# Retention values and gates of a hybrid layer computed as seven block products instead of eight, from block sums of the normalised tokens

## The chip, the cores and the metric

The kernel runs on one core of a Trainium2 chip. The metric is the device time of one execution in microseconds (us). A core has a matrix engine (TensorE, PE in the profile; its weight loads are shown apart as PEld), a vector engine (VectorE, DVE), an activation engine (ScalarE, ACT), GpSimd (POOL) and SyncE (SP). Each engine works through its own instructions in the order in which they stand in its queue; semaphores tie the queues together. SP issues most of the DMA transfers, POOL those that add into their target.

## The reference, cut to what matters

One decoder layer on 512 tokens of width 1024. Of its products with weights, these belong to the retention branch:

```python
h = rms_norm(x, norm_mix)
proj = h @ w_in
rq, rk, rv, rg, cq, ckv, krope, gr, gm = jnp.split(proj, offsets, axis=-1)
rq = rope(rq.reshape(B, S, RET_HEADS, RET_QK_DIM), pos)            # 4 heads of 256
rk = rope(rk.reshape(B, S, RET_HEADS, RET_QK_DIM), pos) * (RET_QK_DIM ** -0.5)
rv = rv.reshape(B, S, RET_HEADS, RET_V_DIM)                        # 4 heads of 512
ro = retention(rq, rk, rv)                                         # decayed causal scores times values
ro = rms_norm(ro, ret_norm.reshape(RET_HEADS, RET_V_DIM)).reshape(B, S, RET_V_W)
a_ret = (ro * jax.nn.silu(rg)) @ w_br
...
mixed = jax.nn.sigmoid(gr) * a_ret + jax.nn.sigmoid(gm) * a_mla
x = x + mixed @ w_o
h2 = rms_norm(x, norm_mlp)
x = x + jnp.square(jax.nn.relu(h2 @ w_up)) @ w_down
```

The values `rv` and the gates `rg` are each a product of the normalised tokens (512 x 1024) with 1024 x 2048 weights. The rest is a latent attention branch (`a_mla`), the output projection `w_o`, the MLP and a gated per-layer embedding.

## The kernel before, in words

**Products.** Tokens lie along the free dimension, features on the 128 partitions. Every float32 product is made of three matmuls on operands split into a high and a low part (`mm3`, L160 to L168; all matmuls are recorded at L165). A split is an ACT copy to the high part and a DVE subtraction that gives the low part (L294 and L295 for activations; L254 and L255 for weights).

**Weights** are streamed in chunks of 128 x 1024 (512 KB). `prepare` (L215 to L240) starts a chunk's transfer on SP into a ring of raw tiles (NRAW = 3), three steps ahead (PREP = 3). `load_chunk` (L243) splits it into a ring of three high and three low tiles (NW = 3), one step ahead (AHEAD = 1). A split therefore waits until the matmuls that used the ring's tile three chunks earlier are done. The order of the work is written out by hand as a list of steps at the end of the kernel (from L1058); one step is one chunk of weights and the matmuls on it. The tile framework orders the work of the engines other than PE from this list.

**The retention stage** is a loop over four heads after the eight `bm` chunks, which project the attention output. For one head h:
- `rq` and `rk`, two chunks each (heads 1 to 3; head 0's run earlier), and four chunks `br` that project the head before;
- `rv`, four chunks (`ret_v`, L692): 24 matmuls a chunk with 128 tokens stationary and 512 weight columns moving;
- the scores `rs` (L705), and `rg` chunks 0 and 1 (`ret_gate`, L743): 24 matmuls a chunk with 128 x 128 weights stationary and 512 tokens moving;
- `ro` (`ret_attend`), `rg` chunk 2, then `so`, the sums of squares of `ro` (`ret_stats`), and `rg` chunk 3;
- between `so` and `pbo`, DVE forms 1/sqrt of the sums in 12 small instructions on 128 x 4 (`mean_rsqrt` and `rsqrt`, L311 to L316, L393). `pbo` (`ret_factor`) is the PE instruction that spreads the result `ro0` over the partitions, and DVE multiplies it into `og` (L741).
- The gate `rg` is multiplied by the tokens' norm factor `rbc` on DVE (`z`, L746), goes through ACT's sigmoid (`sg`, L747) and is multiplied by itself (L748).

The tokens are used as `xg`, which carries the gain but not the norm factor; the factor is multiplied in afterwards (into `rv` as a scale of the split, into `rg` and `gr` by DVE).

**Seven products for eight.** The product with `w_down` (`dn`) already uses a form in which a 2 x 2 block product takes 7 block products of sums of blocks instead of 8: the activations' sums are made on DVE (`combine`), the weights' sums by transfers issued on POOL that add a second chunk into a raw tile that holds the first (L225). The products are numbered 1, 7, 6, 2, 5, 4, 3; the weights of 7, 6, 4 are one tile that is added to twice more, so that its next addition has to wait until the last split has read it.

## Time and profile before

| what | before |
|---|---|
| time, median of 3 runs | 1145.36 us (1144.82 to 1145.98) |
| the profiled execution: time, span of the core | 1144.94 us, 1143.2 us |
| PE, DVE, ACT, POOL busy | 1120.1, 700.0, 484.9, 29.1 us |
| PE instructions | 5300 matmuls, 5300 weight loads in the trace |
| granted TensorE clock, mean | 0.999 |
| DMA | 133.42 MB, mean 117 GB/s |

How to read it: the busy time of PE is near to the span, but matmuls overlap in the pipeline (one of 512 columns is recorded as 0.39 us and the next starts 0.23 us later), so the share says that PE hardly ever stands still and not that its array is full. The chain of work that ended last follows back, from the end, what each step waited for. In a timeline, the first number of a row is its start, the second its recorded duration, and "idle before" how long the engine stood still and what ended it.

### The profile page before, as it was taken

The numbers are of one execution on the slowest core, as the hardware profiler recorded it, in microseconds if no ns is written. First come the engines' busy times: TensorE is split into PE (matmuls) and PEld (weight loads), VectorE is DVE, ScalarE is ACT, GpSimd is POOL, SyncE is SP. The second block draws the span as 40 slices with busy tenths as digits, with TensorE's granted clock in tenths as the row PEclk, the third lists the DMA queues.
The fourth block names the chain that finished last, engine by engine and source line by source line (L and its number), as shares of the span: only waits on it lengthen the run. The fifth ranks groups of instructions, "written<-read, shape, count | busy, mean of one in ns | idle before, by whom it ended". The sixth has DMA issues, their size and how long they took to land.

```text
span 1143.2 us, 13662 instructions
## 1 busy us (share of the span) xinstructions
PE 1120.1 (98%) x5300; PEld 935.0 (82%) x5300; DVE 700.0 (61%) x1138; ACT 484.9 (42%) x682; POOL 29.1 (3%) x38
## 2 busy tenths in 40 slices
PE   7998999999999999999999999999999999999998
PEld 5887878888888888888888888878888888888877
DVE  5777676653448247644834666545566566668675
ACT  6546556452334343233324333424444343445542
POOL 0000000000000000000000000000100001001000
PEclk9999999999999999999999999999999999999999
DMA  6223131233312321331232133676657657667221
GB/s 201 73 69 111 38 89 45 66 111 98 116 56 90 107 89 59 98 117 56 87 110 90 49 105 117 202 248 203 129 167 195 136 175 192 144 204 195 67 90 73
DMA packets 43344, 133.42 MB, mean 117 GB/s; under 512 B 5296, under 2 KB 6576, under 8 KB 43024
## 3 DMA queue, kind: packets, MB, share of 16 engines
q1 hardware_dynamic: 38400, 115.36, 30.5%
q0 software_dynamic: 4736, 17.18, 8.7%
q8 instruction: 41, 0.67, 0.2%
q14 instruction: 23, 0.19, 0.0%
q10 hardware_dynamic: 144, 0.03, 0.0%
HBM read 126.25 MB, written 4.19 MB: 114 GB/s over the span
## 4 chain that ended last, share of the span: by engine, by line
PE 93%; DVE 3%; DMA 2%; ACT 1%; issue 0%; SPq 0%; ACTq 0%; DVEq 0%
PE up L165 15%; PE dn L165 13%; PE rg L165 8%; PE br L165 8%; PE rv L165 8%; PE pg L165 4%; PE rq L165 4%; PE rk L165 4%; PE gr L165 4%; PE bm L165 4%; PE gm L165 3%; PE ro L165 3%; PE wo L165 2%; PE sc L165 2%; PE pcq L165 1%; PE rs L165 1%
## 5 line engine op out<-in xcount | busy, mean ns | idle before, releaser
L254 ACT ACTIVATE wh_dp<-dr 128x1024 fp32r<-128x1024 f32 x56 | 59.4, 1061 | 117.5 <-PE up L165 83.2
L255 DVE TENSOR_TENSOR wl_dp<-dr,wh_dp 128x1024 fp32r<-128x1024 f32 x56 | 68.4, 1221 | 49.9 <-ACT wh_dp L254 49.9
L165 PE MATMUL dn<-wh_dp,cl 128*128 128x512 f32 x224 | 87.2, 389 | 0.0
L165 PE MATMUL dn<-wh_dp,ch 128*128 128x512 f32 x224 | 87.2, 389 | 0.0
L165 PE MATMUL dn<-wl_dp,ch 128*128 128x512 f32 x224 | 87.2, 389 | 0.0
L254 ACT ACTIVATE wh_up<-wr_up 128x1024 fp32r<-128x1024 f32 x32 | 33.9, 1061 | 58.7 <-PE up L165 29.3
L225 POOL DMA_DIRECT2D dr<-wstream x32 | 27.6, 873 | 1028.5 <-DMA dr<-wstream 894.2
L255 DVE TENSOR_TENSOR wl_up<-wr_up,wh_up 128x1024 fp32r<-128x1024 f32 x32 | 39.1, 1222 | 17.8 <-ACT wh_up L254 17.6
L165 PEld LDWEIGHTS dn<-wl_dp,ch 128*128 128x128 f32 x224 | 42.1, 188 | 8.7
L165 PEld LDWEIGHTS dn<-wh_dp,cl 128*128 128x128 f32 x224 | 42.1, 188 | 8.7
L165 PEld LDWEIGHTS dn<-wh_dp,ch 128*128 128x128 f32 x224 | 42.1, 188 | 8.6
L845 DVE SCALAR_TENSOR_TENSOR f<-up,bcx 128x512 f32<-128x512 f32 x32 | 20.6, 685 | 43.9 <-PE up L165 43.9
L255 DVE TENSOR_TENSOR wl_rg<-wr_rg,wh_rg 128x1024 fp32r<-128x1024 f32 x16 | 19.6, 1226 | 36.7 <-ACT wh_rg L254 36.7
L254 ACT ACTIVATE wh_rv<-wr_rv 128x1024 fp32r<-128x1024 f32 x16 | 17.0, 1060 | 55.3 <-PE br L165 26.2
L255 DVE TENSOR_TENSOR wl_rv<-wr_rv,wh_rv 128x1024 fp32r<-128x1024 f32 x16 | 19.6, 1226 | 32.8 <-ACT wh_rv L254 32.8
L254 ACT ACTIVATE wh_rg<-wr_rg 128x1024 fp32r<-128x1024 f32 x16 | 17.0, 1062 | 46.3 <-PE rv L165 35.0
L746 DVE TENSOR_TENSOR z<-rg,rbc 128x512 f32<-128x512 f32 x16 | 11.1, 691 | 39.8 <-PE rg L165 39.8
L254 ACT ACTIVATE wh_br<-wr_br 128x1024 fp32r<-128x1024 f32 x16 | 17.0, 1062 | 41.8 <-issue 18.8
L903 DVE TENSOR_TENSOR d<-d,dn 128x1024 f32<-128x1024 f32 x24 | 29.3, 1219 | 6.5 <-PE dn L165 6.5
L765 DVE TENSOR_TENSOR ret<-ret,br 128x512 f32<-128x512 f32 x24 | 16.5, 686 | 18.2 <-PE br L165 18.1
L622 ACT ACTIVATE p<-p,ng,hr 128x128 f32<-128x128 f32 (+3 forms) x32 | 20.7, 647 | 15.1 <-DVE ng L620 15.1
L255 DVE TENSOR_TENSOR wl_br<-wr_br,wh_br 128x1024 fp32r<-128x1024 f32 x16 | 19.5, 1217 | 3.6 <-ACT wh_br L254 3.6
(1590 smaller groups left out, 3376.9 us busy)
## 6 DMA issues: line engine op xcount, KB each, us to landing
dr<-wstream SPq DMA_DIRECT2D x40, 512.0 KB, 4.3
wr_up<-wstream SPq DMA_DIRECT2D x32, 512.0 KB, 4.2
dr<-wstream POOLq DMA_DIRECT2D x32, 512.0 KB, 5.8
wr_rv<-wstream SPq DMA_DIRECT2D x16, 512.0 KB, 3.4
wr_rg<-wstream SPq DMA_DIRECT2D x16, 512.0 KB, 3.4
wr_br<-wstream SPq DMA_DIRECT2D x16, 512.0 KB, 3.4
wr_gm<-wstream SPq DMA_DIRECT2D x16, 256.0 KB, 2.6
wr_bm<-wstream SPq DMA_DIRECT2D x8, 512.0 KB, 3.5
```

The lines of the kernel that those rows point to most:

```text
L165: return tc.keep_in_program_order(nc.tensor.matmul(*a, **k))
L225: nc.gpsimd.dma_start(raw, chunk(("d", gg, kb, fb, c)), accum_op=ALU.add)
L254: ACT(hi, raw, AF.Copy)
L255: TT(lo, raw, hi.bitcast(F32), op=ALU.subtract)
L622: ACT(cols[b], cols[b], AF.Exp, bias=ng[:, b:b + 1], scale=d["rq"][:, b], accum_out=sums[:, b:b + 1])
L746: TT(z, ps, V["rbc"], op=ALU.mult)
L765: TT(ret[n], ret[n], ps, op=ALU.add)
L845: STT(u[:, i], ps[:, i], 0.0, V["bcx2"], op0=ALU.max, op1=ALU.mult)
L903: TT(to, to, dps[p], op=ALU.add if sign > 0 else ALU.subtract)
```

## The change

**Values.** Two heads are computed together, as 2 x 2 blocks: token halves of 256 by halves of the 1024 features, and feature halves by the two heads' 512 columns. Seven products of two chunks each, 12 matmuls of 512 columns a chunk, for heads 0 and 1 ahead of head 0 and for heads 2 and 3 ahead of head 2. The `br` chunks of head 1 stand between the products of the second pair.

**Gates.** Per head, the 512 gate columns are split into two halves of 256 and the tokens too: seven products of one chunk each, 24 matmuls with 128 x 128 weights stationary and 256 tokens moving. Their order around the other work of the head is 1, 7, `rs`, 2, 6, `ro`, 5, `so`, 4, 3, `pbo`. `seven_out` gathers the results: products 1, 7 and 6 by an ACT copy out of PSUM, 2, 5 and 4 by a DVE addition, and product 3's sum stays in PSUM, where sigmoid and multiplication read it (block 12).

**Tokens.** After each `bm` chunk, `norm_x` loads that eighth of the input again, multiplies it by gain and norm factor on DVE (`xr`) and splits it (`xn`). After the last, `x_operands` forms the block sums for products 7, 6, 5 and 3 (16 DVE instructions of 128 x 256 on tiles `sx` and `sy`) and splits them into tiles that stay on chip (`s70` to `s31`). The multiplications by `rbc` after `rg` and `gr` go away.

**Weights.** 32 chunks of values and gates become 56, and each is split. Those of the products 7, 6, 5 and 4 are summed by adding transfers on POOL. The chunk in product 1 and 4 is split with a negative sign. The ring of raw tiles grows from 3 to 6, that for `w_down` shrinks from 7 to 4.

**Room.** The tiles for activations shrink from 51 to 45. The attention gates (`zm`, later `am`) and the retention sum (`ret`) are stored to DRAM and loaded again (`aside`, `reload`); heads 1 and 2 are added to the stored sum by adding transfers on POOL.

The list of steps is otherwise the same, and PE's instructions up to the last `bm` chunk are the same in number and order. The order of instructions on DVE changes at two places that the prediction speaks of. The first is the start of the first values stage, in the order of DVE. Before, these rows follow each other (`zm7` is the result of the last `bm` chunk, `wl_rv` and `wl_rg` are low parts of weight chunks):

```order
L255 TENSOR_TENSOR wl_rv_0_1_2882<-wr_rv_0_1_2879,wh_rv_0_1_2881 128x1024
L665 TENSOR_TENSOR zm7_2138<-zm7_2138,bm7_2852 128x512
L255 TENSOR_TENSOR wl_rv_0_2_2916<-wr_rv_0_2_2913,wh_rv_0_2_2915 128x1024
L255 TENSOR_TENSOR wl_rv_0_3_2946<-wr_rv_0_3_2943,wh_rv_0_3_2945 128x1024
L255 TENSOR_TENSOR wl_rg_0_0_2976<-wr_rg_0_0_2973,wh_rg_0_0_2975 128x1024
```

Now, from the same place on (`wl_rv070` belongs to product 7's first chunk, `gb7` is what was `zm7`, `s70l` is the low part of the first token sum of product 7):

```order
L267 TENSOR_TENSOR wl_rv070_3064<-wr_rv070_2949,wh_rv070_3063 128x1024
L684 TENSOR_TENSOR gb7_2952<-gb7_2952,bm7_2954 128x512
L697 SCALAR_TENSOR_TENSOR xr7_2983<-xr7_2983,gn_81,rbc_421 128x512
L267 TENSOR_TENSOR wl_rv071_3086<-wr_rv071_3046,wh_rv071_3085 128x1024
L309 TENSOR_TENSOR xn7l_2987<-xr7_2983,xn7h_2986 128x512
L718 TENSOR_TENSOR sx0_2990<-xr0_2670 128x256
L718 TENSOR_TENSOR sx0_2990<-xr1_2714 128x256
L718 TENSOR_TENSOR sx1_2991<-xr2_2758 128x256
L718 TENSOR_TENSOR sx1_2991<-xr3_2802 128x256
L722 TENSOR_TENSOR sy0_3016<-xr0_2670,xr4_2846 128x256
L309 TENSOR_TENSOR s70l_2995<-sx0_2990,s70h_2994 128x512
```

The last eighth of the tokens and five sums now stand between the last `bm` chunk and the operand of product 7; sixteen more rows on the sums (eleven of 128 x 256 and five of 128 x 512) stand between `s70l` and `wl_rv020`, the low part of product 2's first chunk.

The second place is the end of a head, on DVE, ahead of `pbo`. Before, for head 0 (`nt4` and `ro0` are the last steps of 1/sqrt, `z03` reads the last gate chunk out of PSUM):

```order
L314 TENSOR_TENSOR nt4_3252<-ro0_3250 128x4
L315 SCALAR_TENSOR_TENSOR nt4_3252<-nt4_3252,ro0a_3249 128x4
L316 SCALAR_TENSOR_TENSOR ro0_3250<-nt4_3252,ro0_3250 128x4
L746 TENSOR_TENSOR z03_3295<-rg03_3270,rbc_421 128x512
L741 TENSOR_TENSOR og00_3150<-og00_3150,pbo0_3300 128x512
```

Now (`z0_12` is the multiplication of the last gate block by its sigmoid `sg012`, both from product 3's sum in PSUM):

```order
L267 TENSOR_TENSOR wl_rq_1_1_3753<-wr_rq_1_1_3750,wh_rq_1_1_3752 128x1024
L328 TENSOR_TENSOR nt4_3639<-ro0_3637 128x4
L847 TENSOR_TENSOR z0_21_3526<-z0_21_3526,sg021_3680 128x512
L329 SCALAR_TENSOR_TENSOR nt4_3639<-nt4_3639,ro0a_3636 128x4
L330 SCALAR_TENSOR_TENSOR ro0_3637<-nt4_3639,ro0_3637 128x4
L328 TENSOR_TENSOR nt4_3639<-ro0_3637 128x4
L329 SCALAR_TENSOR_TENSOR nt4_3639<-nt4_3639,ro0a_3636 128x4
L847 TENSOR_TENSOR z0_12_3715<-rg01_3355,sg012_3713 128x512
L330 SCALAR_TENSOR_TENSOR ro0_3637<-nt4_3639,ro0_3637 128x4
L267 TENSOR_TENSOR wl_rk_1_0_3788<-wr_rk_1_0_3785,wh_rk_1_0_3787 128x1024
L826 TENSOR_TENSOR og00_3541<-og00_3541,pbo0_3717 128x512
```

The multiplication `z0_12` has moved ahead of the last small step `ro0`, for which `pbo` waits; the same order stands in all four heads.

The diff, cut to its core:

```diff
-NDYN, NKEEP, NW, NRAW, NDRAW, AHEAD, PREP, EARLY, PAD = 51, 16, 3, 3, 7, 1, 3, 1, 104
+NDYN, NKEEP, NW, NRAW, NDRAW, AHEAD, PREP, EARLY, PAD = 45, 16, 3, 6, 4, 1, 3, 1, 104
...
+            nc.sync.dma_start(raw, chunk(("w", blk, kb, fb, c)))
+            dw[blk, "t" if p == 7 else p, c] = raw
+            if p == 7:
+                more(raw, 1, 1)
+            elif p == 5:
+                more(raw, 0, 0)
             return
...
+    def norm_x(k):
+
+        t = T(f"xr{k}")
+        nc.sync.dma_start(t, xT[:, k])
+        STT(t, t, g(G_MIX + k), V["rbc"], op0=ALU.mult, op1=ALU.mult)
+        xr.append(t)
+        xn.append(split(t, f"xn{k}"))
...
+        for p in (7, 6, 5, 3):
+            for c in range(2):
+                t = T(f"sy{c}") if p == 5 else ts[c]
+                for kk in range(2):
+                    k, o = 2 * c + kk, t[:, kk * 256:kk * 256 + 256]
+                    if p == 7:
+                        TT(o, xr[k][:, hi_], xr[k][:, lo_], op=ALU.subtract)
...
+                keep_split(p, c, t)
...
+    CHAIN = {1: "a", 6: "a", 5: "a", 3: "a", 7: "c", 4: "c", 2: "b"}
...
+        if p in (1, 7, 6):
+            to = {1: 11, 7: 22, 6: 21}[p]
+            c[to] = T(f"{name}{to}")
+            ACT(c[to], ps, AF.Copy, scale=1.0 if p == 7 else -1.0)
+            return None
+        if p == 3:
+            return 12, ps
+        to = {2: 11, 5: 22, 4: 21}[p]
+        TT(c[to], c[to], ps, op=ALU.subtract if p == 4 else ALU.add)
+        return to, c[to]
...
+        for k in range(2):
+            for i in range(2):
+                mm3(rvps[ch][i], cut(XS[p][2 * c + k], i * P), cut(w, k * S, S), p in (1, 7, 2) and c + k == 0,
+                    c + k == 2, skip_group_check=True)
...
-        ps = proj(B(f"rg{h}{m}"), xg, w)
-        z, sg = T(f"z{h}{m}"), T(f"sg{h}{m}")
-        TT(z, ps, V["rbc"], op=ALU.mult)
-        tc.keep_in_program_order(ACT(sg, z, AF.Sigmoid))
-        TT(z, z, sg, op=ALU.mult)
...
+        for o in range(2):
+            for k in range(4):
+                mm3(ps[:, o * 256:o * 256 + 256], cut(w, k * 256 + o * P), XS[p][k], p in (1, 7, 2) and o + k == 0,
+                    o == 1 and k == 3, skip_group_check=True)
+        done = seven_out(d.setdefault("z", {}), p, ps, f"z{h}_")
+        if done:
+            blk, z = done
+            sg = T(f"sg{h}{blk}")
+            tc.keep_in_program_order(ACT(sg, z, AF.Sigmoid))
+            if blk == 12:
+                d["z"][12] = T(f"z{h}_12")
+            TT(d["z"][blk], z, sg, op=ALU.mult)
...
         step(("bm", n), branch_m, n)
+        step(None, norm_x, n)
+    step(None, x_operands)
...
+        left = [(("br", h - 1, k), branch_r, h - 1, k) for k in range(4 if h else 0)]
+        for p in (1, 7, 2, 6, 5, 4, 3) if h % 2 == 0 else ():
+            for c in range(2):
+                step(("sw", ("rv", h // 2), p, c), ret_v, h // 2, p, c)
+            if left:
+                step(*left.pop(0))
+        for st in left:
+            step(*st)
+        for p in (1, 7):
+            step(("sw", ("rg", h), p, 0), ret_gate, h, p)
         step(None, ret_scores, h)
-        step(("rg", h, 0), ret_gate, h, 0)
-        step(("rg", h, 1), ret_gate, h, 1)
+        for p in (2, 6):
+            step(("sw", ("rg", h), p, 0), ret_gate, h, p)
         step(None, ret_attend, h)
-        step(("rg", h, 2), ret_gate, h, 2)
+        step(("sw", ("rg", h), 5, 0), ret_gate, h, 5)
         step(None, ret_stats, h)
-        step(("rg", h, 3), ret_gate, h, 3)
+        for p in (4, 3):
+            step(("sw", ("rg", h), p, 0), ret_gate, h, p)
         step(None, ret_factor, h)
         step(None, ret_gated, h)
```

162 lines of the change are left out of this document (105 added, 57 removed).

## The prediction

> **What bounds the kernel now.** I read the page first: busy times, and the chain that ended last by engine and line.
>
> ```profile
> PE 1120.1 (98%) x5300; PEld 935.0 (82%) x5300; DVE 700.0 (61%) x1138; ACT 484.9 (42%) x682; POOL 29.1 (3%) x38
> ...
> PE 93%; DVE 3%; DMA 2%; ACT 1%; issue 0%; SPq 0%; ACTq 0%; DVEq 0%
> PE up L165 15%; PE dn L165 13%; PE rg L165 8%; PE br L165 8%; PE rv L165 8%; PE pg L165 4%; PE rq L165 4%; PE rk L165 4%; PE gr L165 4%; PE bm L165 4%; PE gm L165 3%; PE ro L165 3%; PE wo L165 2%; PE sc L165 2%; PE pcq L165 1%; PE rs L165 1%
> ```
>
> The end is set by PE for 93% of the span; `rv` and `rg`, which the change touches, are 8% each. Next the chain in order of time over head 0 (start, duration, work), and two stretches of the retention stage with PE, PEld, DVE, ACT and POOL busy, the granted clock, DMA share and GB/s.
>
> ```profile
> 287.08 21.76 PE rv L165 x96
> 308.84 3.85 PE rs L165 x24
> 312.69 10.91 PE rg L165 x48
> 323.60 7.71 PE ro L165 x48
> 331.31 5.46 PE rg L165 x24
> 336.77 0.79 PE so L165 x8
> 337.56 5.61 PE rg L165 x24
> 343.16 0.44 PE pbo L165 x4
> ```
>
> ```profile
> 280.00:345.00 65.00, 65.00 (x315) 55.15 (x314) 28.30 (x47) 21.78 (x30) 0.00 (x0) 1.00 0.25 85
> ...
> 476.00:700.00 224.00, 224.00 (x1043) 188.16 (x1042) 128.32 (x191) 76.03 (x102) 0.00 (x0) 1.00 0.26 88
> ```
>
> The chain through a head is PE alone, piece on piece, PE stands still nowhere, and DVE is busy for 44% of the first stretch. So every matmul less is time won, and every new wait of PE is time lost in full.
>
> **What it removes.** Values go from 384 matmuls of 512 columns to 336. One costs 21.76/96 = 0.2267 us (row of `rv`): 48 x 0.2267 = 10.9 us. Gates go from 384 of 512 columns (87.1 us) to 672 of 256. For those the scores of head 0 have twelve in a row, the first and the last of which are
>
> ```profile
> 311.10 0.28 PE L165 MATMUL rs<-rqx0h,rkx0l 128*128 128x256 f32 x1
> ...
> 312.41 0.28 PE L165 MATMUL rs<-rqy0h,rky0h 128*128 128x256 f32 x1
> ```
>
> 11 steps in 1.31 us, 0.119 us each, with a new weight tile each time, as the gates will have. 672 x 0.119 = 80.0 us, 7.0 us less (7 eighths of 87.1 would be 76.2; the pitch is a little over half). Gain: **17.9 us**.
>
> The row of a weight load, from the group of the `dn` product, speaks to that pitch:
>
> ```profile
> L165 PEld LDWEIGHTS dn<-wl_dp,ch 128*128 128x128 f32 x224 | 42.1, 188 | 8.7
> ```
>
> A load is recorded as 188 ns, longer than the pitch of 119 ns, so loads overlap the matmuls in the rows above. The Trainium skill ("TensorE: Matmul & The Clock Gate", sections "LDWEIGHTS (loading the stationary operand)" and "The mechanism") gives a load about 128/1.2 = 107 ns and says that it overlaps matmuls in flight only when the row group differs; by that, as an estimate, a gate matmul would take 107 + 119 = 226 ns, the gates 152 us, and the change would lose. The trace's rows contradict it, and the sum goes by the rows; what is left of the doubt is a rival below.
>
> **What it adds off PE.** 24 more chunks to split, each by a copy on ACT and a subtraction on DVE:
>
> ```profile
> L255 DVE TENSOR_TENSOR wl_rv<-wr_rv,wh_rv 128x1024 fp32r<-128x1024 f32 x16 | 19.6, 1226 | 32.8 <-ACT wh_rv L254 32.8
> L254 ACT ACTIVATE wh_rg<-wr_rg 128x1024 fp32r<-128x1024 f32 x16 | 17.0, 1062 | 46.3 <-PE rv L165 35.0
> ```
>
> A chunk now lasts 12 x 0.2267 = 2.72 us (values) or 24 x 0.119 = 2.86 us (gates) on PE, over twice a split on either engine: free in the steady state. It is not free where DVE has other work in a row. Two such places are in the order of DVE.
>
> **Cost A, the token sums, once.** What followed the last `bm` matmul before:
>
> ```profile
> 286.91 0.39 PE L165 MATMUL rv<-wh_rv,xg0l 128*128 128x512 f32 x1
> ```
> ```profile
> 287.11 1.06 ACT L254 ACTIVATE wh_rv<-wr_rv 128x1024 fp32r<-128x1024 f32 x1 [4.38 <-PE bm L165]
> ```
> ```profile
> 287.11 0.69 DVE L665 TENSOR_TENSOR zm<-zm,bm 128x512 f32<-128x512 f32 x1 [3.12 <-PE bm L165]
> 288.21 1.23 DVE L255 TENSOR_TENSOR wl_rv<-wr_rv,wh_rv 128x1024 fp32r<-128x1024 f32 x1 [0.41 <-ACT wh_rv L254]
> ```
>
> With T the start of the first values matmul, the freed weight tile is filled by ACT from T+0.2, and DVE can subtract from T+1.3. For the steps of DVE, ACT and PE I use the distances between neighbouring rows at the end of head 0 and of two 256-column instructions elsewhere:
>
> ```profile
> 155.47 0.42 DVE L616 CUSTOM_DVE_ANT_0 p<-sc,kf 128x256 f32<-128x256 f32 x1
> 155.81 0.08 DVE L616 DVE_READ_ACCUMULATOR2_ANT mx<- 128x1 f32 x1
> ```
> ```profile
> 337.59 0.16 DVE L393 TENSOR_SCALAR ro0a<-so 128x4 f32<-128x4 f32 x1
> ...
> 337.90 1.22 DVE L255 TENSOR_TENSOR wl_rq<-wr_rq,wh_rq 128x1024 fp32r<-128x1024 f32 x1
> 339.04 0.68 DVE L748 TENSOR_TENSOR z<-z,sg 128x512 f32<-128x512 f32 x1
> 339.64 0.16 DVE L312 TENSOR_SCALAR ro<-ro 128x4 int32<-128x4 int32 x1
> ...
> 341.22 0.16 DVE L315 SCALAR_TENSOR_TENSOR nt<-nt,ro0a 128x4 f32<-128x4 f32 x1
> 341.41 0.16 DVE L316 SCALAR_TENSOR_TENSOR ro<-nt,ro 128x4 f32<-128x4 f32 x1
> 343.20 0.69 DVE L746 TENSOR_TENSOR z<-rg,rbc 128x512 f32<-128x512 f32 x1 [1.62 <-PE rg L165]
> ```
> ```profile
> 336.81 1.06 ACT L254 ACTIVATE wh_rq<-wr_rq 128x1024 fp32r<-128x1024 f32 x1 [4.29 <-PE rg L165]
> 337.77 0.62 ACT L747 ACTIVATE sg<-z 128x512 f32<-128x512 f32 x1
> ```
> ```profile
> 342.77 0.39 PE L165 MATMUL rg<-xg7h,wh_rg 128*128 128x512 f32 x1
> 343.00 0.60 PE L165 MATMUL pbo<-cst,ro 128*128 128x128 f32 x4
> ```
>
> So 1.14 us for 1024 columns, 0.60 for 512, 0.34 for 256, 0.2 for a small step, on ACT 1.0 and 0.62. DVE's order after T: `wl_rv070` from 1.3 to 2.4, `gb7` and `xr7` to 3.6. `wl_rv071` needs the tile that product 1's first chunk frees at T+2.9 and ACT's copy until 4.0, so it ends at 5.2; `xn7l` 5.8, five sums 7.5, `s70l` 8.2. PE has only the two chunks of product 1 until T+5.44, so it waits 2.8 us for product 7. Then stand, ahead of `wl_rv020`, 11 x 0.34 + 5 x 0.60 = 6.7 us of sums and splits, and its own 1.14: T+16.0, or 16.3 where ACT's halves of those splits come last. PE is done with product 7 at 8.2 + 5.44 = 13.6: it waits 2.6 us more. Product 5 adds into the PSUM of product 6 right behind ACT's copies out of it, with no product between: the first copy starts when its PSUM's last matmul ends, three matmuls (0.68 us) before product 6 does, and takes 0.62 plus the 0.39 that a matmul is recorded for: 0.3 us. After that a values chunk needs 1.14 us of DVE in 2.72, and the second pair has `br` chunks between and its token sums ready. Cost A: **5.8 us**. Bounds: 3 if the scheduled distances are shorter than the single rows, 9 if the last eighth of the input (`xr7`), which SP issues behind the store of `am6`, lands late too.
>
> **Cost B, the end of each head.** Before, DVE's last `ro` ended at 341.6, under the last gate chunk, and `pbo` followed the last gate matmul after 0.23 us: no wait. Now `z0_12` stands ahead of the last `ro`, and it needs the sigmoid of product 3's sum: from the last gate matmul's end 0.04 us to ACT, 0.62 there, 0.04 to DVE, 0.60 there, `ro` 0.2, and 0.1 until `pbo`: 1.6 to 1.7 us in which PE has nothing else, since `rq` stands behind `pbo`. Besides, DVE has less time for what stands between `so` and `pbo`: products 4 and 3 last 5.7 us as the one chunk did, but there are 12 small steps (2.4 us), two weight splits (2.3) and four instructions on 512 columns (2.4), 7.1 us, which alone would end 1.4 us late. The two together, in DVE's order with the wait for product 4 to end: 2.1. I take **2.0 us for each of four heads, 8.0**; bounds 6.4 and 9.
>
> **What I cost at nothing.** The adding transfers on POOL: they are the unknown here, since the retention stage had none. Their rows are those of `dn`:
>
> ```profile
> dr<-wstream POOLq DMA_DIRECT2D x32, 512.0 KB, 5.8
> ```
> ```profile
> DMA to landing us min/median/max: 5.3/5.8/10.8
> ```
> ```profile
> q1 hardware_dynamic: 38400, 115.36, 30.5%
> q0 software_dynamic: 4736, 17.18, 8.7%
> ```
>
> Tightest is the gates' shared tile: addition for product 6 starts when `wl_rg070` is done, about 1 us after product 1 begins; 5.8 us of transfer and 2.1 of split end 8.9 us after it. PE gets there at 3 x 2.86 + 3.85 = 12.4 us. But in heads 0 and 2 the score splits stand behind that split on DVE, 5.6 us of them ahead of `ro`, which PE reaches at 15.3: slack 0.8 us there, 3.5 elsewhere. In odd heads most of the scores' work stands behind it too, but some ahead. The stores, additions and reloads of `ret` and the reloads of `am` lie in the heads and behind them, with DMA at 25%; the products and softmax ahead of `bm` keep PE's order, with `kq` weights loading somewhat earlier and four DVE multiplications more: 0, give or take 1 us.
>
> **The sum.** -17.9 + 5.8 + 8.0 = -4.1 us, on the profiled execution's 1144.9: 1140.8. Its time is 0.4 us under the runs' median of 1145.36, so the median becomes **1141.3 us**. About 0.2% (2.3 us) is what a measurement of this kernel can tell from no change.
>
> **The rivals.**
>
> *The waits are hidden (0.16).* If DVE and ACT run ahead of PE more than I think (a split earlier by one ring tile, sums started while `bm` still runs), A and B shrink to a third or less and the gain of 17.9 us comes through: -18 to -10, 1127 to 1135. For it: DVE is busy for only 44% of that stretch. Against: both waits follow from the order within DVE's queue, not from its load.
>
> *Slower: additions land late (0.22).* The queue rows give an adding transfer 8.7% of 1143.2 us by 32.8 chunks' worth (17.18 MB), 3.0 us of all 16 DMA engines, a plain chunk 30.5% by 220 chunks' worth, 1.6. Over the `bm` chunks and the first values stage (8 x 24 + 168 matmuls of 0.2267, 82 us) I count 8 `bm` chunks, 24 transfers of 256 KB, 10 plain and 8 adding transfers for the values and the first of the gates: 12.7 + 19 + 16 + 24 + 6 = 78 us. DMA, 25% busy in the stretch above, is nearly full there. If additions then land after 10.8 us, the longest above, `ro` starts 10.8 - 5.8 - 0.8 = 4.2 us late in heads 0 and 2, and product 6 about 1.5 us late in heads 1 and 3: +11.4, net +7, **1152 us**. It decides against the change by more than 0.2% from landings of 9.6 us on (6.4 us to be lost). Against it: in the heads themselves DMA has room, and `dn`, which takes such additions now, runs without idle time ahead of its matmuls (last column):
>
> ```profile
> L165 PE MATMUL dn<-wl_dp,ch 128*128 128x512 f32 x224 | 87.2, 389 | 0.0
> ```
>
> The Trainium skill ("DMA: Bandwidth & Descriptors", section "Measured (HBM→SBUF, 128 partitions, SWDGE, issued from GpSimd)") fits 2.0 us + bytes/436e3 to such transfers, by estimate 3.2 us here; the trace's 5.8 is more, and stands.
>
> *Gates paced by weight loads (0.02).* Were 672 loads of 0.188 us the pace, the gates would take 126.3 us, 39 more than before: 1187. The rows of `rs` speak against it.
>
> *Costs eat the gain (0.08).* A and B at their upper bounds, 18 us: 1145, no change.
>
> **How the numbers follow.** My forecast has 0.52, its own range -9 to -1 us, of which 0.06 lies within 0.2%. Faster: 0.46 + 0.16 = 0.62; same: 0.06 + 0.08 + 0.02 of the slow rival where landings are between = 0.16; slower: 0.22 with the gates' rival. The range leaves out the faster half of the first rival (0.08), the third rival and what goes past the second's price: 1131 to 1151.
>
> **What would show it.** In the changed profile: twelve gate matmuls in 1.4 us; `rv` pieces of 2.72 us; PE waiting 2 to 3 us for DVE's `s70l` and again for `wl_rv`, once; PE waiting about 2 us for `ro0` ahead of each `pbo`, DVE's `z` before it; no PE wait for a chunk's split behind a POOL transfer. PE waits elsewhere of over 3 us, or none at `pbo`, make it wrong.

## The result, and the profile after

The changed kernel takes 1155.16 us, the median of 5 runs (1150.85 to 1155.62), against 1145.13 us for the kernel before on the same chip (5 runs, 1144.44 to 1145.98): 1.0081 times as long, 95% interval 1.0062 to 1.0100. The forecast was 1141.3 us, 4.1 us faster. The change is 10 us slower. The profiled execution took 1155.40 us, its span is 1153.6 us against 1143.2, and its mean granted clock is 0.991 against 0.999.

The page of the changed kernel, busy times, and the shares of the chain that ended last:

```profile
PE 1110.3 (96%) x5540; PEld 939.6 (81%) x5540; DVE 737.8 (64%) x1205; ACT 537.0 (47%) x762; POOL 70.7 (6%) x86
...
PE 88%; DVE 5%; DMA 3%; ACT 2%; issue 2%; SPq 0%; POOL 0%; ACTq 0%; POOLq 0%; DVEq 0%
```

PE does less work (1110 us against 1120), but its share of the chain falls from 93% to 88%: other engines and transfers now set the end in places. The table shows where. It takes the start of the first matmul of each stage from PE's timeline in both traces.

| stage | before, us | after, us | after - before |
|---|---|---|---|
| start of the span to first `bm` matmul | 243.39 | 251.98 | +8.6 |
| `bm` | 43.52 | 43.52 | 0 |
| first values stage | 2 x 21.76 = 43.5 | 295.50 to 345.00 = 49.5 | +6.0 |
| second values stage, with the `br` chunks between | 2 x 21.76 + 21.76 = 65.3 | 480.13 to 541.37 = 61.2 | -4.0 |
| the rest of the four heads, up to `wo` | | | +0.9 |
| `wo` to the end | | | -1.1 |

(Before, the values were computed head by head, so two of its values pieces of 21.76 us stand for one stage of now.) The heads have two large terms that cancel, as will be seen. What PE waited for (what waits, for what; total us, times, longest):

```profile
PE rv L172 <- DVE s70l L309: 8.4, 1, 8.4
PE pbo L172 <- DVE ro L330: 6.6, 4, 1.7
...
PE pt0a L172 <- ACT q2h L311: 3.5, 1, 3.5
PE pA L172 <- ACT xg1h L311: 2.9, 1, 2.9
PE sqr L172 <- DVE sa L557: 2.1, 1, 2.1
```

The first two are forecast waits. The other three are not: they lie ahead of the `bm` chunks, in code that the change does not touch. Before, `xg1h` and `sqr` cost PE no wait that the view lists, and `pt0a` waited 0.8 us. One wait of before is gone:

```profile
PE pk L165 <- DVE wl_kq L255: 2.2, 2, 1.7
```

**Ahead of `bm`.** PE's 1213 matmuls up to the first one of `bm` are the same in both traces and stand in the same order, so each can be set beside itself (starts in us):

| first matmul of | before | after | later by |
|---|---|---|---|
| the second token tile (`xg1`) | 10.06 | 12.13 | 2.1 |
| the fourth token tile (`xg3`) | 17.84 | 19.60 | 1.8 |
| `sc` | 89.23 | 91.00 | 1.8 |
| `pk`, behind it | 94.89 | 94.75 | -0.1 |
| `pt0a` | 103.55 | 105.26 | 1.7 |
| the next `pbk` | 123.03 | 127.60 | 4.6 |
| `sqr` | 150.78 | 157.61 | 6.8 |
| the `pbk` behind it | 164.80 | 173.42 | 8.6 |

The tokens make PE 1.8 us late. At `pk` it catches up, since the `kq` weights are there earlier, but `pt0a` hangs on DVE and ACT, which are still late (DVE's first row of `p` starts at 98.02 instead of 95.77). So PE waits there in one piece of 3.5 us, is as late as it was at the tokens, and loses 2.9 us more in what follows, which the clock below explains. The wait for `sqr` adds 2.2 us and the stretch behind it 1.8.

**The gates.** The chain through head 0 now, to be set beside the one of before:

```profile
345.16 5.75 PE rg L172 x48
350.92 3.88 PE rs L172 x24
354.80 5.76 PE rg L172 x48
```

Two products of 24 matmuls take 5.75 us, 0.120 us a matmul; the forecast was 0.119. And these pieces follow each other without a gap. The product gain is there: per head 168 x 0.120 = 20.1 us instead of 21.76, and 5.4 us from each values stage, together about 17.4 us of the 17.9.

**The end of a head**, in DVE's order, and then on PE with its weight loads:

```profile
378.44 0.16 DVE L329 SCALAR_TENSOR_TENSOR nt<-nt,ro0a 128x4 f32<-128x4 f32 x1
378.52 0.68 DVE L847 TENSOR_TENSOR z<-rg,sg 128x512 f32<-128x512 f32 x1
379.12 0.15 DVE L330 SCALAR_TENSOR_TENSOR ro<-nt,ro 128x4 f32<-128x4 f32 x1
```
```profile
377.38 0.28 PE L172 MATMUL rg<-s31l,wh_rg 128*128 128x256 f32 x1
377.39 0.19 PEld L172 LDWEIGHTS rg<-s31h,wh_rg 128*128 128x128 f32 x1
377.50 0.28 PE L172 MATMUL rg<-s31h,wh_rg 128*128 128x256 f32 x1
...
379.42 0.62 PE L172 MATMUL pbo<-cst,ro 128*128 128x128 f32 x4 [1.63 <-DVE ro L330]
```

The multiplication by the last sigmoid stands one place ahead of the last small step, and PE waits 1.63 us for that step, and 1.6 to 1.7 in each of the four heads. That is Cost B.

**The start of the first values stage**, the chain that ended last (start, duration, work):

```profile
296.39 0.38 SPq L681
...
296.87 7.79 DMA xr<-xT
...
305.36 1.22 DVE wl_rv L267
306.57 0.60 DVE xn7l L309
307.17 1.34 DVE sx L718 x4
...
308.85 0.61 DVE s70l L309
...
309.51 3.22 PE rv L172 x7
...
316.30 1.23 DVE wl_rv L267
...
317.57 10.95 PE rv L172 x47
```

DVE goes through the rows in the forecast order (`wl_rv071`, `xn7l`, the sums, `s70l`), and the last row but one is the split of `wl_rv020` that PE waits for next (0.6 us, where the forecast had 2.6). But it can start only when the last eighth of the tokens has landed. SP issues that transfer at 296.87, right behind the store of one gate block and the reload of the next, and it takes 7.79 us; the same kind of transfer takes 4.0 us in the median over the kernel. This is the case that the forecast kept as its upper bound. The chain has one more oddity: seven matmuls of 512 columns take 3.22 us, 0.46 each, which is twice the 0.2267 of before.

**The clock.** Two-microsecond windows (busy PE, PEld, DVE, ACT, POOL; granted clock; DMA share; GB/s):

```profile
106.00:108.00 2.00, 2.00 (x10) 1.90 (x9) 1.36 (x3) 2.00 (x5) 0.00 (x0) 0.50 0.17 24
...
110.00:112.00 2.00, 2.00 (x8) 1.58 (x7) 0.27 (x1) 0.56 (x1) 0.00 (x0) 0.68 0.03 8
...
306.00:308.00 2.00, 0.00 (x0) 0.00 (x0) 2.00 (x5) 1.17 (x3) 0.85 (x1) 0.50 1.06 239
...
310.00:312.00 2.00, 2.00 (x6) 1.54 (x6) 2.00 (x7) 0.90 (x2) 0.00 (x0) 0.50 1.00 199
```

After the waits of 3.5 and 8.4 us PE gets half its clock, and keeps it for a while after it is at work again (from 105.26 and 309.5). So a long wait is paid for twice: behind `pt0a` PE falls 2.9 us further back, behind `sqr` 1.8 (table above), and the seven matmuls behind `s70l` lose 3.22 - 7 x 0.2267 = 1.6 us. DMA is at its limit in those rows around 306 to 312. Over the whole values stage:

```profile
295.70:345.20 49.50, 40.47 (x170) 32.35 (x169) 36.99 (x56) 27.43 (x37) 6.93 (x9) 0.93 0.78 201
```

The `bm` chunks ahead of it run at full clock with DMA at 80%, and PE loses nothing there. In the values stage PE is busy for 40.5 us of 49.5, at a mean clock of 0.93.

### The profile page after: what moved, and what is told of

Read it like the earlier page. It is cut to its first block, busy times and chain, and to the rows that moved or that the text cites. A ratio compares the mean times of both kernels' runs of the same rounds, so it can differ in the third digit from the quotient of the medians.

```text
span 1153.6 us, 14652 instructions
## 1 busy us (share of the span) xinstructions
PE 1110.3 (96%) x5540; PEld 939.6 (81%) x5540; DVE 737.8 (64%) x1205; ACT 537.0 (47%) x762; POOL 70.7 (6%) x86
## 4 chain that ended last, share of the span: by engine, by line
PE 88%; DVE 5%; DMA 3%; ACT 2%; issue 2%; SPq 0%; POOL 0%; ACTq 0%; POOLq 0%; DVEq 0%
PE up L172 15%; PE dn L172 13%; PE br L172 8%; PE rv L172 5%; PE rg L172 5%; PE pg L172 4%; PE rq L172 4%; PE rk L172 4%; PE gr L172 4%; PE wo L172 3%; PE bm L172 3%; PE gm L172 3%; PE ro L172 3%; PE sc L172 2%; DMA wr_rg<-wstream 2%
## 5 line engine op out<-in xcount | busy, mean ns | idle before, releaser
L172 PE MATMUL dn<-wh_dn,cl 128*128 128x512 f32 x224 | 87.2, 389 | 0.0
L172 PE MATMUL dn<-wh_dn,ch 128*128 128x512 f32 x224 | 87.2, 389 | 0.0
L172 PE MATMUL dn<-wl_dn,ch 128*128 128x512 f32 x224 | 87.1, 389 | 0.0
L265 ACT ACTIVATE wh_dn<-wr_dn 128x1024 fp32r<-128x1024 f32 x32 | 34.0, 1062 | 75.5 <-PE up L172 54.3
L267 DVE TENSOR_TENSOR wl_dn<-wr_dn,wh_dn 128x1024 fp32r<-128x1024 f32 x32 | 39.1, 1221 | 27.4 <-ACT wh_dn L265 27.4
L267 DVE TENSOR_TENSOR wl_rg<-wr_rg,wh_rg 128x1024 fp32r<-128x1024 f32 x20 | 24.5, 1225 | 40.5 <-ACT wh_rg L265 40.2
L172 PEld LDWEIGHTS dn<-wh_dn,ch 128*128 128x128 f32 x224 | 42.0, 188 | 8.8
L172 PEld LDWEIGHTS dn<-wh_dn,cl 128*128 128x128 f32 x224 | 42.0, 188 | 8.7
L172 PEld LDWEIGHTS dn<-wl_dn,ch 128*128 128x128 f32 x224 | 42.0, 188 | 8.6
L265 ACT ACTIVATE wh_dn<-dr_dn 128x1024 fp32r<-128x1024 f32 x24 | 25.4, 1060 | 42.5 <-PE up L172 29.2
L267 DVE TENSOR_TENSOR wl_dn<-dr_dn,wh_dn 128x1024 fp32r<-128x1024 f32 x24 | 29.4, 1223 | 22.4 <-ACT wh_dn L265 22.4
L265 ACT ACTIVATE wh_rv<-wr_rv 128x1024 fp32r<-128x1024 f32 x28 | 29.4, 1057 | 17.9 <-PE rv L172 6.3
```

The lines of the kernel that those rows point to most:

```text
L172: return tc.keep_in_program_order(nc.tensor.matmul(*a, **k))
L265: ACT(hi, raw, AF.Copy, scale=sign)
L267: TT(lo, raw, hi.bitcast(F32), op=ALU.subtract)
```

## The experiments

**The theories.** T1: the time comes from the two forecast waits, Cost A larger than thought and Cost B. T2: it comes from what the change borrowed, tiles and buffers, far from the edited products: the deeper ring of raw tiles and the 45 activation tiles put work ahead of the `bm` chunks in another order. T3, the rival of the prediction: adding transfers land late. The table of stages gives T1 6.0 + 5.4 = 11.4 us in the first values stage (38.1 us would be 168 matmuls of 0.2267) and 6.6 in the heads, T2 8.6 us ahead of `bm`; T3 could be a part of the 11.4. Differences below are between the medians on one chip.

### Is it the borrowed room?

**The kernel before with a deeper ring** (and with 47 tiles, since the ring takes room):

```diff
-NDYN, NKEEP, NW, NRAW, NDRAW, AHEAD, PREP, EARLY, PAD = 51, 16, 3, 3, 7, 1, 3, 1, 104
+NDYN, NKEEP, NW, NRAW, NDRAW, AHEAD, PREP, EARLY, PAD = 47, 16, 3, 5, 5, 1, 3, 1, 104
```

> The kernel before with 5 raw weight tiles in place of 3 (47 activation tiles in place of 51, 5 tail tiles in place of 7), nothing else. Theory: the changed kernel lost 8.6 us before its first bm chunk because a deeper raw ring lets SP put weight chunks ahead of the input tokens and of the small query transfers; then this kernel's bm chunks start 2 to 8 us later than 243.6 us too and its time is 1147 to 1153. Rival: the loss came from the stores of the attention gates or from fewer activation tiles; then the time stays within 1.5 us of the kernel before.

Measured: 1156.07 us against 1145.82, ratio 1.0091 (1.0074 to 1.0107); its first `bm` matmul starts at 255.42 instead of 243.39. Not one product was changed, and the kernel is as slow as the changed one, slower than either expectation. But three numbers were changed (the ring, the tiles and the ring for `w_down`), so the run doesn't say which.

**Tiles alone:**

```diff
-NDYN, NKEEP, NW, NRAW, NDRAW, AHEAD, PREP, EARLY, PAD = 51, 16, 3, 3, 7, 1, 3, 1, 104
+NDYN, NKEEP, NW, NRAW, NDRAW, AHEAD, PREP, EARLY, PAD = 47, 16, 3, 3, 7, 1, 3, 1, 104
```

> The kernel before with 47 activation tiles in place of 51, its three raw tiles kept. Theory: what the ring of raw tiles does not explain of the loss ahead of bm (3.7 us with the ring as before, of 8.6) comes from the fewer activation tiles, seen as a wait of 2 us at the query norm of the second group; then its bm chunks start 2 to 4 us later than 243.4 us and the time is 1148 to 1150. Rival: those 3.7 us come from the stores of the attention gates; then this kernel takes 1145 to 1146.5.

Measured: 1157.18 against 1145.14, ratio 1.0107 (1.0089 to 1.0125), `bm` at 259.39; both expectations were too low. Four tiles fewer cost all of it here, so the run before says nothing of the ring. Nor is this the price in the changed kernel, which takes the attention gates out of the tiles.

**Tiles in the room that the change leaves.** Two kernels that are the one before, with the attention gates stored and loaded again as the change does; one with 45 tiles, one with 51:

```diff
-            zm[n] = T(f"zm{n}")
-            TT(zm[n], gate_ps[n], V["rbc"], op=ALU.mult)
+            t = T(f"zm{n}")
+            TT(t, gate_ps[n], V["rbc"], op=ALU.mult)
+            zm[n] = spill.tile([P, S], F32, tag=f"zm{n}", name=f"zm{n}d")
+            nc.sync.dma_start(zm[n], t)
...
+        t = T(f"gb{n}")
+        nc.sync.dma_start(t, zm[n])
+        zm[n] = t
```

> The kernel before with the attention gates stored to DRAM and loaded again ahead of bm and 45 activation tiles, its ring of three raw tiles kept: what the changed kernel does ahead of bm but for the deeper ring. Theory: the fewer tiles and the stores cost what the changed kernel still lost with the ring as before, 3.7 us; bm starts at 247 us, the time is 1148 to 1150. Rival: nothing is lost without the deeper ring, 1145 to 1146.5.

> The same with all 51 activation tiles. Theory: the loss comes from the number of tiles, which changes the order of DVE at the second group's query norm; with 51 it goes, and the time is 1145 to 1146.5. Rival: the stores and loads make it, and it stays at 1148 to 1150.

Measured: with 51 tiles 1145.88 against 1145.47, ratio 1.0008 (0.9998 to 1.0018), so the stores and reloads cost nothing; with 45 tiles 1150.19, ratio 1.0037 (1.0024 to 1.0051), `bm` at 247.16. Tiles cost about 4 us. With 45, PE has the wait ahead of `sqr` that the changed kernel has:

```profile
PE sqr L165 <- DVE sa L541: 2.1, 1, 2.1
```

With 51 it is not in the list. `sqr` multiplies `sa`, which DVE ends at 152.6 with 45 tiles and at 148.6 with 51: with 45, the rows ahead of it on ACT and DVE stand idle for 2.0 and 1.5 us until a matmul of `sc` has run. That makes 3.8 of the 8.6 us (`bm` at 247.16 against 243.39), half of it in the wait and half in the half-clock stretch behind it; the rest must be in what else differs there.

**The order of the loads.** SP's queue in the first 14 us (start, duration, what is issued), of the kernel before:

```profile
1.65 2.95 SPq L240 DMA_DIRECT2D wr_a<-wstream  x3
4.64 0.43 SPq L345 DMA_DIRECT2D x<-xT  x1
8.68 0.80 SPq L240 DMA_DIRECT2D wr_a<-wstream  x2
9.54 0.43 SPq L345 DMA_DIRECT2D x<-xT  x1
...
11.67 2.32 SPq L345 DMA_DIRECT2D x<-xT  x5
```

and of the changed one:

```profile
1.64 3.67 SPq L247 DMA_DIRECT2D wr_a<-wstream  x6
5.36 0.59 SPq L365 DMA_DIRECT2D x<-xT  x1
...
9.94 0.34 SPq L247 DMA_DIRECT2D wr_cq<-wstream  x1
10.33 0.42 SPq L365 DMA_DIRECT2D x<-xT  x1
...
13.74 2.34 SPq L365 DMA_DIRECT2D x<-xT  x5
```

The first token tile goes out at 1.18 in both. With six raw tiles free instead of three, weight chunks go out ahead of the other tokens, which PE needs first: the second token tile is issued at 5.36 instead of 4.64 and lands at 11.33 instead of 8.99, and the last five go out 2 us later. The same happens later with weight chunks and the small query transfers. The last of these lands at 91.4 instead of 90.0, which is less than the 1.8 us that everything there is late by, and PE doesn't wait for them; what comes of it is that the `kq` weights are early, and that PE's idle time falls into the one long wait for `pt0a`. Three kernels go after it.

*Ring of three as before, a second ring of three for product 7, chunks from `bm` on issued in the order of the list:*

```diff
+            elif p == 7:
+                raw = wpool.tile([P, 1024], F32, tag="wsum", name="wr_" + nm, bufs=3)
...
-            nc.sync.dma_start(raw, chunk(("w", blk, kb, fb, c)))
+            tc.keep_in_program_order(nc.sync.dma_start(raw, chunk(("w", blk, kb, fb, c))))
```

> The changed kernel with its six raw tiles as two rings, three for ordinary chunks and three for the tiles that are added to (product 7), and the chunks from bm on issued in the list's order, so that SP's order ahead of bm is that of the kernel before but for the stores of the attention gates. Theory: the first bm chunk starts at 243 to 245 us and not at 252, 1147 us if the values stage is unchanged (3 us either way for the shorter ring). Rival: the stores or the fewer activation tiles made the loss; bm starts at 250 or later and the time stays above 1152.

Measured: `bm` starts at 247.08, between the two expectations and as with 45 tiles alone. So the 4.9 us between 247.1 and 252.0 go with the ring of six. They are single profiles: three kernels below that leave the code ahead of `bm` as the change has it start `bm` at 253.34, 253.85 and 256.25, so the step is 5 to 9 us. The whole is no better, 1156.26, ratio 1.0090 (1.0073 to 1.0108): the first values stage takes 46.4 us, but the second one 64.8 instead of 61.2, and PE waits for weight chunks there (2.0 and 0.8 us). Most of what it saves early it gives back later.

*Nine early chunks held behind the transfers that they overtook:*

```diff
+        behind = {("a1", 7): "x7", ("cq", 0): "x7", ("cq", 1): "x7", ("kq", 2): "qp0", ("kq", 3): "qp0",
+                  ("gm", 4, 0): "qp0", ("v", 3): "qp1", ("gm", 7, 1): "qp1", ("rq", 0, 0, 0): "qp1"}.get(key)
+        if behind:
+            with tc.issue_after(last[behind]):
+                nc.sync.dma_start(raw, chunk(key))
```

> The changed kernel with its six raw tiles, and nine weight transfers ahead of bm held behind the transfers that they followed in the kernel before: three behind the last input tokens, six behind the small query transfers of their group. Theory: the deeper ring costs 4.9 us ahead of bm only because these transfers go first; bm starts at 247 us, the rest is as in the changed kernel, 1150 to 1151. Rival: the order of the transfers is not it, bm starts at 250 us or later and the time stays at 1153 to 1156.

Measured: 1154.45 against 1145.69, ratio 1.0076 (1.0060 to 1.0092). `bm` starts at 254.60 in its profile and the wait for `xg1h` is still 3.1 us: three more chunks stood ahead of the tokens. The numbers are the rival's, but the order of before was not yet reached, so this decides nothing.

*All twelve:*

```diff
+        behind = {("a1", 4): "x1", ("a1", 5): "x1", ("a1", 6): "x2", ("a1", 7): "x7", ("cq", 0): "x7", ("cq", 1): "x7", ("kq", 2): "qp0", ("kq", 3): "qp0",
+                  ("gm", 4, 0): "qp0", ("v", 3): "qp1", ("gm", 7, 1): "qp1", ("rq", 0, 0, 0): "qp1"}.get(key)
```

> The changed kernel with all twelve weight transfers ahead of bm behind those that they followed in the kernel before, so that SP's order there is that of the kernel before but for the stores of the gates (in loads_in_order the second and third input token tiles still came behind four weight chunks, and PE waited 3.1 us for the second). Theory: the deeper ring costs only by that order; first products of cq at 28 to 29 us, bm at 247 us, 1150 to 1151. Rival: bm at 250 us or later, and 1153 or more.

Measured: 1151.99 against 1145.06, ratio 1.0063 (1.0047 to 1.0078), about 3 us better than the change and between the two expectations. `bm` starts at 249.53, `pt0a` waits 0.8 us as before, and `xg1h` still 2.4. The order of the loads is a cause, worth about 3 us. Set beside the kernel before as in the table, PE is 2.0 us late behind the first tokens and 2.1 at `pt0a`: it waits 2.2 us for `kq` weights and 0.8 at `pt0a` again, and the half-clock stretch behind `pt0a` is gone. So what the order gains is that stretch. The 2.0 us at the tokens stay: the second token tile is issued at 3.06, earlier than before, and lands at 11.28 instead of 8.99. SP's order is that of before, but its times are not; the next two weight chunks go out at 3.5 and 4.0, where the ring of three let them go at 8.7 and 9.2. No run holds those two back, so it is not shown that they are the cause.

*Two rings of three of another cut, products 1 and 7 in the second, held behind a `bm` chunk:*

```diff
+                tag = "wsum" if p in (1, 7) else "wraw"
+                raw = wpool.tile([P, 1024], F32, tag=tag, name="wr_" + nm, bufs=NRAW)
+            with tc.issue_after(V["bm"]):
+                nc.sync.dma_start(raw, chunk(("w", blk, kb, fb, c)))
```

> The changed kernel with two rings of three raw tiles, products 1 and 7 in the second, and the first of these transfers held behind that of the sixth bm chunk; the others are free. Theory: the first bm chunk starts at 247 us as with the rings before, and the values stage is no worse than in the changed kernel, so 1150 to 1152. Rival: with three tiles for products 2, 5 and 3 the values stage waits for transfers, and the time stays at 1154 to 1157.

Measured: 1164.24 against 1145.14, ratio 1.0157 (1.0134 to 1.0181). Both expectations missed. The profile is of its fastest run, 1158.80: `bm` starts at 249.12, so a third of the early loss is gone, but the values stage takes 50.9 us, still with a wait of 8.2 us for `s70l`. Its chain holds an adding transfer of 11.8 us.

### Is it the two forecast waits?

**Cost B alone.** The last two multiplications by the sigmoid, and the low parts of the `rq` and `gr` chunks, are held behind the last `ro`:

```diff
+            if blk in (21, 12):
+                with tc.issue_after(V["ro"]):
+                    TT(d["z"][blk], z, sg, op=ALU.mult)
```

> The changed kernel with the multiplications of gate blocks 21 and 12 and the splits of the next two weight chunks put behind the last step of 1/sqrt on DVE. Theory: each of the four waits of 1.6 us ahead of pbo goes, 6.6 us in all, 1148.5 us. Rival: DVE has too little time there and the work only moves, so PE waits for the split of the next chunk instead: 2 us or less gained.

Measured: 1150.88 against 1145.82, ratio 1.0053 (1.0033 to 1.0073), 4 to 5 us better than the change. That is between the two expectations. No wait ahead of `pbo` is left and the end of each head, from its last two gate products on, is 1.8 to 1.9 us shorter, 7.4 in all; head 2 gives 0.7 back in waits ahead of `ro`. Cost B is what the prediction said it is. The profile is of the slowest of the four runs (1155.34) and has a longer wait for `s70l`, 13.1 us.

**Cost A alone.** The tokens are loaded and normalised two `bm` chunks earlier, and their sums stand behind `bm` chunks 1, 3 and 5:

```diff
+        for k in (0, 1, 2) if n == 0 else (n + 2,) if n < 6 else ():
+            step(None, norm_x, k)
...
-        step(None, norm_x, n)
-    step(None, x_operands)
+        if n in (1, 3, 5):
+            step(None, x_operands, {1: ((7, 0), (7, 1)), 3: ((6, 0), (5, 0), (3, 0)), 5: ((6, 1), (5, 1), (3, 1))}[n])
```

> The changed kernel with the tokens loaded and normalised two bm chunks earlier and the block sums made while bm still runs. Theory: the wait of 8.4 us for the first sum of product 7, the slow clock behind it and the wait for product 2 go, 9 to 11 us, about 1145 us. Rival: DMA is the bound of that stretch, and PE then waits as long for the chunks that are added by transfers: 3 us or less gained.

Measured: 1150.75 against 1145.82, ratio 1.0042 (1.0029 to 1.0055), between the two expectations. The second stage is at its full gain (59.8 us, before 65.3); the first one falls only from 49.5 to 46.5, though `s70l` is waited for no more. What PE waits for there, and the chain up to the end of that wait and behind it:

```profile
PE rv L172 <- DVE wl_rv L267: 4.8, 3, 4.0
```
```profile
294.00 4.14 DMA gb<-zm4d
...
299.44 0.68 DVE s71l L309
...
305.88 1.14 DVE wl_rv L267
...
307.07 3.96 PE rv L172 x10
...
312.35 8.80 DMA wr_rv<-wstream
```

The wait of 4.0 us ends at 307.07, and it is still DVE's order: DVE stood behind the reload of a stored gate block (`zm4`) until 298.8, and then the sums and splits from 299.44 on kept it from the split `wl_rv`, which stands behind them. Half clock follows (ten matmuls in 3.96 us). The adding transfer, 8.8 us from its issue to its landing, comes after that, ahead of two waits of 0.6 and 0.5 us. So T1 holds the larger part of this stage even now, and T3 a small one.

**Without the adding transfers** (the products 7, 6, 5 and 4 of values and gates then have one block where they need a sum):

```diff
-                nc.gpsimd.dma_start(raw, chunk(("w", blk, kb, fb, c)), accum_op=ALU.add)
+                if blk[0] == "dn":
+                    nc.gpsimd.dma_start(raw, chunk(("w", blk, kb, fb, c)), accum_op=ALU.add)
```

> The changed kernel without the adding transfers for values and gates, so the weights' sums are left out there. Theory: of the 11.4 us that the values stage lost, what goes beyond DVE's own work (5.8 us predicted) and the 3.3 us of head 2 come from the additions and the DMA traffic that they make: 1145 to 1148. Rival: the order of the loads of the last tokens behind the stores makes the loss, whatever the additions do: 1151 to 1155.

Measured: 1150.90 against 1145.14, ratio 1.0049 (1.0035 to 1.0062), 4.3 us better than the change and between the two expectations, just under the rival's 1151. The first stage takes 45.4 us, 4.1 less. Its wait and its window:

```profile
PE rv L172 <- DVE s70l L312: 3.3, 1, 3.3
```
```profile
299.80:345.20 45.40, 41.63 (x170) 33.15 (x169) 36.31 (x53) 27.16 (x37) 0.00 (x0) 0.92 0.41 139
```

With DMA at 41% instead of 78%, the last eighth of the tokens lands in 4.5 us instead of 7.8, and DVE's order alone gives a wait of 3.3 us, near the forecast 2.8. So the additions and the room that they take on DMA make about 4 us of the 11.4; 7.3 stay, with DVE's order and the clock (0.92 of full over the stage) in them. The heads change by 0.4 us, in head 2: the additions cost next to nothing there.

Five of these kernels have this stage's list as the change has it. Side by side, the wait follows the landing of the last eighth of the tokens:

| kernel | last eighth, issue to landing, us | wait for `s70l`, us | first values stage, us |
|---|---|---|---|
| without additions | 4.5 | 3.3 | 45.4 |
| loads_exact | 7.4 | 7.8 | 49.4 |
| the change | 7.8 | 8.4 | 49.5 |
| loads_in_order | 9.4 | 10.0 | 52.2 |
| factor_first | 11.5 | 13.1 | 55.2 |

### Versions that put the parts together

**Two rings that share, with both waits mended:** ring_two with the second ring given to products 7, to the second chunks of products 2 and 3 and to the gates' product 1, `w_down`'s second chunks too, with factor_first and tokens_early.

```diff
+                second = c == 1 if blk[0] == "dn" else p == 7 or (p, c) in ((2, 1), (3, 1)) or (blk[0], p) == ("rg", 1)
+                raw = wpool.tile([P, 1024], F32, tag="wsum" if second else "wraw", name="wr_" + nm, bufs=NRAW)
```

> The changed kernel with two rings of three raw tiles shared so that the values stage has all six, the gate blocks behind the last step of 1/sqrt, and the tokens loaded two bm chunks earlier with their sums made under bm. Theory: 1155.2 less 4.9 (ring ahead of bm), 4.3 (1/sqrt, as measured) and 4.4 (tokens, as measured) is 1141.6, below the kernel before. Rival: the values stage is bound by DMA and takes back what is won ahead of it, as it did with the first pair of rings: 1148 or more.

Measured: 1156.04 against 1145.47, ratio 1.0090 (1.0074 to 1.0105). The expectation missed. PE now waits for gate weights, and the chain names the transfer:

```profile
PE rg L172 <- DVE wl_rg L274: 9.9, 2, 5.3
```
```profile
337.21 7.78 DMA wr_rg<-wstream
```

This is T3 in the heads, where the prediction had put it. In the change itself PE waits for no gate chunk.

**Two rings, both waits mended, with the tokens loaded from ACT's queue and product 7 of the gates computed first:**

```diff
-        nc.sync.dma_start(t, xT[:, k])
+        nc.scalar.dma_start(t, xT[:, k])
...
-        for p in (1, 7):
+        for p in (7, 1):
```

> The changed kernel with the two rings, the gate blocks behind the last step of 1/sqrt, product 7 ahead of product 1 in the gates, and the tokens loaded two bm chunks earlier on ACT's queue with their sums made under bm. Theory: the losses add up, so taking them away does too: 1155.2 - 4 (rings) - 5 (1/sqrt) - 2 (head 2) - 6 (tokens) = 1138. Rival: DMA is the bound of the values stage and what is won ahead of it is lost there: 1144 to 1150.

Measured: 1153.90 against 1145.14, ratio 1.0082 (1.0065 to 1.0099): missed by 16 us. The values stage takes 51.8 us, with 6.3 us of waits for `wl_rv`. The longest of them, 4.5 us, ends at 304.17 behind a nearly unbroken row of sums and splits on DVE, as with early tokens. From 297.0 on the chain goes mostly through transfers of `wr_rv`, the longest of them an adding one:

```profile
319.80 11.55 DMA wr_rv<-wstream
```

T1 and T3 both hold this stage, and the two edits of this run didn't help against them.

**One ring of six, nine loads in order, with factor_first and tokens_early:**

> The same with the gate blocks behind the last step of 1/sqrt and the tokens loaded two bm chunks earlier. Theory, with losses that add up where no DMA bound is met: bm at 247 us, a values stage of 46.5 us as with early tokens alone, four heads 1.6 us shorter each: 1155.2 - 4.9 - 4.3 - 4.4 = 1141.6. Rival: DMA gives the time back as a wait for added weight chunks in the heads, as it did with the two rings: 1146 or more.

Measured: 1140.89 (1139.73 to 1145.12) against 1145.69, ratio 0.9958 (0.9944 to 0.9972). The expected time held, but one of its three terms did not: `bm` starts at 252.65 and not at 247, in a profile of the slowest run.

**The same with all twelve loads:**

> The same with the gate blocks behind the last step of 1/sqrt and the tokens loaded two bm chunks earlier. Theory: bm at 247 us in place of 252.7, 3 to 5 us less than the 1140.9 of loads_factor_tokens, 1136 to 1138. Rival: the order of the first token tiles does not matter, or the DMA-bound values stage takes it back, 1140 to 1142.

Measured: 1140.95 (1139.40 to 1142.84) against 1145.06, ratio 0.9966 (0.9953 to 0.9978). Its lower expectation missed; the rival's time, 1140 to 1142, came true. Both are faster than both kernels, and with one ring of six the values stage still takes 46.3 us:

```profile
293.30:339.50 46.20, 41.06 (x169) 32.38 (x168) 35.05 (x50) 26.87 (x38) 6.87 (x8) 0.96 0.95 242
```
```profile
PE rv L172 <- DVE wl_rv L276: 4.5, 3, 4.0
```

DMA is 95% busy there, but the longest wait is not for an added chunk. As with early tokens alone, DVE gets from the reload of `zm4` (landed at 294.64) through the sums to the split `wl_rv` at 302.37, PE waits 4.0 us for that, and half clock follows. Wait and clock make nearly 6 of the 8 us above the 38.1 that the stage's matmuls need; the rest goes in waits of 0.5 us and less, some of them behind an adding transfer in the chain. That DMA bounds the stage is not shown. In this kernel the heads end 3.0 us earlier than before (`wo` at 700.48 against 703.53).

## Why the prediction was wrong, point by point

*What bounds the kernel.* Right: PE sets the end, and each wait of PE was paid in full. The forecast's own tests, PE waits elsewhere of over 3 us and a wait for `s70l` outside 2 to 3 us, both came out against it (3.5 us ahead of `pt0a`; 8.4).

*The gain, 17.9 us.* Right: 17.4, with a pitch of 0.120 us. The doubt whether each weight load paces its matmul is settled: at the end of the head above, a load recorded as 0.19 us lies beside matmuls 0.12 us apart, so the rival of 1187 us is out. The prediction's estimate of 226 ns a matmul rests on the Trainium skill ("TensorE: Matmul & The Clock Gate", sections "LDWEIGHTS (loading the stationary operand)" and "The mechanism"). The trace, with 120 ns, does not agree with it.

*Cost B, 8.0 us.* Right in mechanism, a little large in size: 1.63 us a head, 6.6 in all, at the lower bound of 6.4. The estimate that small steps alone would end 1.4 us late was not needed; the wait for the sigmoid alone accounts for it. Removing it gave 4.3 us in the medians and 7.4 us at the ends of the heads, of which head 2 lost 0.7 again.

*Cost A, 5.8 us, bounds 3 to 9.* The mechanism was right and the size was not: 11.4 us, over the upper bound, in the first stage, and 1.4 us in the second. The first stage's 11.4 us are 8.4 of waiting for `s70l` (forecast 2.8), 0.6 of waiting for `wl_rv` (forecast 2.6), 1.6 lost to half clock and 0.8 in steps around them; the 1.4 of the second stage are a wait of 0.8 us for `wl_rv` and its neighbours, and the other kernels with one ring of six have at most 0.4 us of it. The last eighth of the tokens landed 7.8 us after its issue, which the forecast had only as a bound, and without the additions the stage is 4.1 us shorter. With the additions gone the wait for `s70l` is 3.3 us, so the counting of DVE's rows was good; what it was started from was not. Of the clock the forecast said nothing.

*The step that failed.* "The products and softmax ahead of `bm` keep PE's order, with `kq` weights loading somewhat earlier and four DVE multiplications more: 0, give or take 1 us." They cost 8.6 us. PE's order was indeed kept, and the `kq` weights were indeed earlier. But DVE's order changed there too, beyond the two places that the account of the change names (two splits of `kq` weights, at 85.25 and 88.80, stand among the small steps of `hr` now). The shrinking of the tiles from 51 to 45 cost about 4 us there (before_aside45 against before_aside51). The ring of six cost another 4.9 us by its profiles, since SP then issues weight chunks ahead of input tokens: 1.7 us of it come from the late tokens and 2.9 from the half clock behind `pt0a`, where PE's idle time falls into one long wait (loads_exact, which puts the loads back, gains 3.2 us in the median and 2.4 of the 8.6). The account of the change lists both numbers of the diff; the prediction priced neither. Without this step, with the sizes as measured, the sum is -17.4 + 11.4 + 1.4 + 6.6 = +2.0 us: no gain, but not 10 us of loss.

How much of the 8.6 us is the clock can be read from the table of PE's starts: 2.9 us behind `pt0a` and 1.8 behind `sqr`, so more than half. A half-clock stretch is not always lost time, though: before_aside51 has two, and starts `bm` at 243.76 and takes 1145.88 us. What stays open ahead of `bm` is why the second token tile lands late even with the loads in the order of before (2.0 us, two profiles: `bm` at 249.53 and 249.77).

*The rival "additions land late", 1152 us.* Its time was near the one measured by luck: its place was wrong, and most of the loss came from elsewhere. In the heads, where it was put, the change shows no wait for a gate chunk. In the first values stage, where its own count of DMA (78 us of transfers in 82) had stood, the additions cost 4 us. The landing times that it feared are there, in the rows of the DMA issues (KB each, median us to landing):

```profile
wr_rv<-wstream POOLq DMA_DIRECT2D x16, 512.0 KB, 7.9
wr_rg<-wstream POOLq DMA_DIRECT2D x16, 512.0 KB, 6.2
```

The prediction's estimate of 3.2 us rests on a fit that stands in the section "Anatomy of one DMA — SWDGE (gpsimd) path" of the Trainium skill's page "DMA: Bandwidth & Descriptors", and not in the section that it names. The rows above are two to two and a half times as long.

*The rival "the waits are hidden".* It did not come true by itself, and half of it did by hand: with tokens and sums early, `ro` first and the loads in order, the kernel takes 1141 us. That this is also the forecast number is chance: it is made of 17.4 us of gain, no Cost B, 8 us in the values stage instead of 5.8, and 6.4 us ahead of `bm` that the forecast did not have, less what the end of the kernel gives.
